# Modulation sums of a two-layer diffusion backbone: ScalarE products and accumulating transfers in place of VectorE sums

## The chip, the core and the metric

The kernel runs on one core of a Trainium2 chip. A core has a matrix engine (TensorE, PE in the profile; its weight loads are listed as PEld), VectorE (DVE), ScalarE (ACT), GpSimd (POOL) and SyncE (SP), each with an instruction stream of its own that is worked off in order; they wait for each other through semaphores. Transfers are issued from an engine's queue and carried by 16 DMA engines that all queues share. The metric is the device time of one execution in microseconds.

## What is computed

Two layers over 512 latent and 256 context tokens of width 1024: bidirectional retention, then a chunked gated MLP. Before each layer the tokens are normalised and modulated with shift, scale and gate, which come from a conditioning vector:

```python
silu_c = jax.nn.silu(c)
for i in range(DEPTH):                                   # DEPTH = 2
    shift_x, scale_x, gate_x = jnp.split(silu_c @ ada_w[i] + ada_b[i], 3, axis=-1)
    hx = rmsnorm(x, norm_g[i]) * (1 + scale_x[:, None]) + shift_x[:, None]
    ...                                                  # i = 0: retention, i = 1: gated MLP
    x = x + gate_x[:, None] * out_x
return rmsnorm(x, final_g)
```

All is float32. The products `silu_c @ ada_w` that are not needed at once, layer 0's gate and layer 1's shift, scale and gate (1024 columns each), are the subject here.

## The kernel before, in words

In the large matrix products each operand is split into a high and a low part, and three partial products are summed: a weight tile `raw` (128x1024) comes in, ScalarE casts it to the high part of `hl`, VectorE subtracts to get the low part, and PE multiplies both (24 matmuls of 128x256 per tile and product). Products are grouped seven to a quad, by a scheme that saves one product in eight; some tiles are differences of two raw ones, formed on VectorE in place. After products ScalarE copies PSUM banks to `snap` tiles (11 buffers), which GpSimd's queue stores to DRAM (`spill`, line 142). SyncE's queue brings in all weights (`load`, line 145), in order.

Beside this main work runs a generator, `background` (line 882), a step at a time (`step`, line 927, called from the loop over quads at line 1044, and from `attend` and `project_out`). It works in four pieces: gate of layer 0, shift, scale and gate of layer 1. In each, `ada_piece` (line 846) brings eight rows of 128x1024 weights (`adag_d`, 512 KB each) into slots `bg`, two to a piece, one load per step, and adds them up, each scaled by a column of `cpad` (one number per partition), in the tile `a` (`ada_a` in the profile). The sum over the 128 partitions follows on PE in `columns` (line 864) for pieces 0 to 2: matmuls of `ones` with `a` into PSUM, a copy to `cole`, transposes, a copy to `gate0`, `sh1` or `gs1`. Piece 3 casts and splits `a` into `ada_h` and multiplies that by ones. Piece 3 runs with the attention of heads 0 and 1 and uses the slots `w2` and `w3`, pieces 0 to 2 run with the projections and use `g2` and `g3`, with `a` in `g1`.

What sets the order: a scheduler lays out each engine's stream before the run by its own estimates. Matmuls keep the order of the text. On ScalarE and VectorE an instruction of a background step is held behind the one before it in the text (`aside`, line 920), the rest is free. SyncE's and GpSimd's streams are laid out freely; where a load's slot isn't free yet, the queue waits there, and what stands behind waits with it.

In `attend` (line 1060) `score` makes `pf` on VectorE, ScalarE casts it to `ph`, VectorE subtracts `pl`; PE multiplies both with `v`; `finish` sums squares and `gated` makes `gt`, which PE transposes.

Of the kernel before, what the change touches and what calls it, by code (L numbers as in the profile page):

```python
# [9 lines left out]
AF = mybir.ActivationFunctionType  # L10
ALU = mybir.AluOpType
# [56 lines left out]
def hybrid_kernel(ctx, tc, xT_d, cT_d, cv_d, sv_d, rows_d, ada0_d, adag_d, w_d, rope_d, dec_d, ws_d, id_d, out_d):  # L68
    nc = tc.nc
    pe, act, dve, sp = (Queue(tc, e) for e in (nc.tensor, nc.scalar, nc.vector, nc.sync))  # L70
# [11 lines left out]
    def st(shape, tag, dt=F32, bufs=1, name=None):  # L82
        return sb.tile(shape, dt, tag=tag, name=name or tag, bufs=bufs)
# [60 lines left out]
    def load(dst, src):  # L144
        sp.dma_start(dst, src)
# [340 lines left out]
    cpad = st([P, KT, 32], "cpad")  # L486
# [355 lines left out]
    def bg_raw(tags):  # L842
        spot[0] += 1
        return st([P, 1024], tags[spot[0] % len(tags)], name="bg")

    def ada_piece(i, tag, tags):
        a = st([P, D], tag, name="ada_a")
        rows = []
        for k in range(KT + 1):
            if k < KT:  # L850
                rows.append(bg_raw(tags))
                load(rows[k], adag_d[8 * i + k])
            if k == 0:
                yield None
                continue
            r, c = rows[k - 1], cpad[:, k - 1, 0:1]
            if k == 1:
                dve.tensor_scalar(a, r, c, None, ALU.mult)
            else:
                dve.scalar_tensor_tensor(a, r, c, a, ALU.mult, ALU.add)  # L860
            yield None
        yield a

# [18 lines left out]
    def background():  # L882
        for i in range(4):
            a = None
            for a in ada_piece(i, *(("g1", ("g2", "g3")) if i < 3 else ("oA22", ("w2", "w3")))):
                if a is None:
                    yield
# [750 lines left out]
```

## Time and profile before

| | |
|---|---|
| time, median of 3 runs | 871.4 us (870.92 to 871.57) |
| the profiled execution, first to last instruction | 869.6 us |
| granted clock of TensorE over the span, mean | 0.998 |
| bytes moved by DMA | 153.81 MB, mean 177 GB/s |
| ScalarE casts of 128x1024 weights `hl<-raw` | 197, 203.0 us in all |

In the profile a row of a timeline has start, length, engine, line, operation, out<-in, shapes, how many, and in brackets the idle time before it and what ended it. Nearly all instructions have line 54, since a helper records them; they are told apart by the names of their tiles. A row of a tile's answer has the shortest, median and longest duration in ns, and the first and last start. A DMA row has the queue that issues it, the number, the size, and the median time from issue to landing. "SPq L54 <- DVE x" tells what SyncE's queue waited for: us in all, times, longest.

### The profile page before, as it was taken

What the parts mean: (1) busy time and instruction counts of PE and PEld (TensorE: products, weight loads), DVE (VectorE), ACT (ScalarE), POOL (GpSimd) and SP (SyncE); (2) the same over time, 40 slices, a digit from 0 to 9 for tenths busy, and PEclk for the clock granted to TensorE, in tenths of its full rate; (3) what the DMA queues carried; (4) which work ended last, traced back from release to release, by engine and by line L of the source; (5) the groups of instructions that cost most, each with busy time, mean ns of one, the idle gap of its engine ahead of it and who ended that gap; (6) DMA issues with size and microseconds to landing.
All of it is one profiled execution on the core that took longest, in us unless ns stands there. A gap on an engine that the chain in (4) does not pass through costs nothing.

```text
span 869.6 us, 16989 instructions
## 1 busy us (share of the span) xinstructions
PE 860.9 (99%) x6898; PEld 824.1 (95%) x6898; DVE 715.0 (82%) x1004; ACT 458.5 (53%) x711; POOL 58.3 (7%) x96
## 2 busy tenths in 40 slices
PE   8999999999999999999999999999999999999997
PEld 7899999999999999999989899999999899899986
DVE  4799988699789777878676679999899488688995
ACT  5476644435544346627363549744666456255434
POOL 0001210101102011000000002011000000000110
PEclk9999999999999999999999999999999999999999
DMA  9943887557567467746164602635435035035522
GB/s 359 404 152 109 256 279 254 170 181 242 203 213 256 132 219 302 267 165 241 66 222 141 215 4 110 211 117 206 135 122 193 26 122 203 16 122 170 120 46 102
DMA packets 74238, 153.81 MB, mean 177 GB/s; under 512 B 7728, under 2 KB 32816, under 8 KB 74160
## 3 DMA queue, kind: packets, MB, share of 16 engines
q1 hardware_dynamic: 65856, 128.40, 43.7%
q0 software_dynamic: 7872, 24.12, 8.2%
q8 instruction: 54, 0.88, 0.4%
q14 instruction: 24, 0.20, 0.1%
q10 hardware_dynamic: 432, 0.20, 0.1%
HBM read 128.58 MB, written 24.12 MB: 176 GB/s over the span
## 4 chain that ended last, share of the span: by engine, by line
PE 95%; DMA 3%; DVE 1%; ACT 0%; issue 0%; SPq 0%; DVEq 0%; ACTq 0%
PE pst L54 95%; DMA ada_w<-in_ada_dram 2%; DMA xs<-in_xT_dram 1%; DVE o L54 0%; ACT junk L54 0%; SPq L54 0%; ACT fss L54 0%; ACT o L54 0%; DVE fss L54 0%; ACT oA L54 0%; DVE oA L54 0%; DVE xs L54 0%; DVEq L1634 0%; DVE gs L54 0%; DVE ada_s L54 0%
## 5 line engine op out<-in xcount | busy, mean ns | idle before, releaser
L54 DVE TENSOR_TENSOR hl<-raw,hl 128x1024 fp32r<-128x1024 f32 (+2 forms) x197 | 235.4, 1199 | 65.9 <-ACT hl L54 65.3
L54 ACT CAST hl<-raw 128x1024 fp32r<-128x1024 f32 (+2 forms) x197 | 203.0, 1034 | 137.9 <-DVE raw L54 55.8
L54 PE MATMUL pst<-hl,oS 128*128 128x256 f32 x1152 | 133.9, 277 | 0.0
L54 PEld LDWEIGHTS pst<-hl,oS 128*128 128x128 f32 x1152 | 132.4, 188 | 0.4 <-issue 0.4
L54 PE MATMUL pst<-oS,hl 128*128 128x256 f32 x1104 | 132.5, 277 | 0.0
L54 PEld LDWEIGHTS pst<-oS,hl 128*128 128x128 f32 x1104 | 128.1, 188 | 0.8 <-issue 0.8
L54 PE MATMUL pst<-oA,hl 128*128 128x256 f32 x936 | 116.5, 279 | 0.1
L54 PEld LDWEIGHTS pst<-oA,hl 128*128 128x128 f32 x936 | 110.6, 188 | 2.3 <-issue 0.8
L54 DVE TENSOR_TENSOR raw<-raw 128x1024 f32<-128x1024 f32 x92 | 111.8, 1219 | 0.8
L54 ACT COPY snap<-pst 128x512 f32<-128x512 f32 x92 | 53.7, 584 | 92.7 <-PE pst L54 92.4
L54 PE MATMUL pst<-hl,oA 128*128 128x256 f32 x768 | 92.4, 277 | 0.0
L54 PE MATMUL pst<-og,hl 128*128 128x256 f32 x768 | 91.1, 278 | 0.0
L54 PEld LDWEIGHTS pst<-og,hl 128*128 128x128 f32 x768 | 89.2, 188 | 0.3
L54 PEld LDWEIGHTS pst<-hl,oA 128*128 128x128 f32 x768 | 89.4, 188 | 0.0
L54 PE MATMUL pst<-v,ph 128*128 128x512 f32 x192 | 59.8, 393 | 0.0
L54 PE MATMUL pst<-hl,ya 128*128 128x512 f32 (+1 forms) x246 | 59.1, 386 | 0.0
L54 PEld LDWEIGHTS pst<-hl,ya 128*128 128x128 f32 x246 | 45.3, 188 | 9.5
L54 DVE TENSOR_TENSOR snap<-pst,snap 128x512 f32<-128x512 f32 x69 | 47.3, 685 | 5.3 <-PE pst L54 5.3
L54 PE MATMUL pst<-hl,hc 128*128 128x256 f32 x384 | 46.1, 276 | 0.0
L54 PEld LDWEIGHTS pst<-hl,hc 128*128 128x128 f32 x384 | 44.7, 188 | 0.0
L54 ACT CAST ph<-pf 128x512 fp32r<-128x512 f32 x24 | 14.8, 618 | 54.5 <-DVE pf L54 54.1
L54 PEld LDWEIGHTS pst<-v,ph 128*128 128x128 f32 x192 | 36.1, 188 | 7.1
(186 smaller groups left out, 1022.7 us busy)
## 6 DMA issues: line engine op xcount, KB each, us to landing
raw<-in_w_dram SPq DMA_DIRECT2D x224, 256.0 KB, 4.1
bg<-in_adag_dram SPq DMA_DIRECT2D x32, 512.0 KB, 3.9
ada_w<-in_ada_dram SPq DMA_DIRECT2D x16, 512.0 KB, 8.7
raw<-in_w_dram SPq DMA_DIRECT2D x16, 512.0 KB, 4.3
bg<-in_dec_dram SPq DMA_DIRECT2D x12, 512.0 KB, 4.8
v<-snap POOLq DMA_DIRECT2D x16, 256.0 KB, 5.5
z<-snap POOLq DMA_DIRECT2D x16, 256.0 KB, 4.7
v<-v SPq DMA_DIRECT2D x8, 512.0 KB, 3.4
```

The costliest lines, as they stand in the source:

```text
L54: made = op(*args, **kw)
```

## The change

Row 0 is loaded into the tile of the sum itself and scaled there by ScalarE; rows 1 to 7 are scaled in place by ScalarE, and each is added to the sum by a transfer of GpSimd's queue that accumulates into it, from SBUF to SBUF.

```diff
             if k < KT:
-                rows.append(bg_raw(tags))
+                rows.append(a if k == 0 else bg_raw(tags))
                 load(rows[k], adag_d[8 * i + k])
-            if k == 0:
-                yield None
-                continue
-            r, c = rows[k - 1], cpad[:, k - 1, 0:1]
-            if k == 1:
-                dve.tensor_scalar(a, r, c, None, ALU.mult)
-            else:
-                dve.scalar_tensor_tensor(a, r, c, a, ALU.mult, ALU.add)
+            if k:
+                r = rows[k - 1]
+                act.activation(r, r, AF.Copy, scale=cpad[:, k - 1, 0:1])
+                if k > 1:
+                    nc.gpsimd.dma_start(a, r, accum_op=ALU.add)
             yield None
```

The streams shift at many places; three are shown. The number behind a tile's name is that of the buffer's use and differs between the two programs. The first is GpSimd's queue during piece 0, before (`v`, `vc`, `q` and `z` are stores of the projections of heads 0 and 1), with what each waits for (DMASW: an earlier transfer of this queue, DMAHW: a load of SyncE's):

```order
L142 DMA vc1_220<-snap_1698 256x1x256 [waits DMASW7_49,Activation_49]
L142 DMA q01_192<-rope_a_1771 128x512 [waits DMASW0_49,DVE_49]
L142 DMA z11_226<-snap_1596 256x1x256 [waits DMASW1_49,Activation_49]
L142 DMA z10_225<-snap_1638 256x1x256 [waits DMASW2_49,Activation_49]
L142 DMA v11_214<-snap_1809 256x1x256 [waits DMASW3_49,Activation_49]
L142 DMA v10_213<-snap_1843 256x1x256 [waits DMASW4_49,DVE_49]
```

and after:

```order
L142 DMA vc1_220<-snap_1697 256x1x256 [waits DMASW7_49,Activation_49]
L857 DMA ada_a_1564<-bg_1604 128x1024 [waits DMASW0_49,DMAHW0_49,PE_49,Activation_49]
L142 DMA q01_192<-rope_a_1771 128x512 [waits DMASW1_49,DVE_49]
L142 DMA z11_226<-snap_1595 256x1x256 [waits DMASW2_49,Activation_49]
L142 DMA z10_225<-snap_1637 256x1x256 [waits DMASW3_49,Activation_49]
L857 DMA ada_a_1564<-bg_1700 128x1024 [waits DMASW4_49,DMASW0_49,Activation_49]
L142 DMA v11_214<-snap_1810 256x1x256 [waits DMASW5_49,Activation_49]
L857 DMA ada_a_1564<-bg_1778 128x1024 [waits DMASW6_49,DMASW4_49,Activation_49]
L857 DMA ada_a_1564<-bg_1813 128x1024 [waits DMASW7_49,DMASW6_49,Activation_49]
L857 DMA ada_a_1564<-bg_1872 128x1024 [waits DMASW7_49,Activation_49]
L142 DMA v10_213<-snap_1845 256x1x256 [waits DMASW1_49,DVE_49]
```

Five transfers of the sum stand between stores that followed each other before, and each waits for the transfer of the row before it.

The second is ScalarE's stream during piece 2, in the projections of head 2 and 3, before (casts of weights, and copies of PSUM banks that PE writes to again later):

```order
L54 CAST hl_3288<-raw_2836 128x1024
L54 CAST hl_3381<-raw_3114 128x1024
L54 COPY snap_3349<-pst_3322 128x512
L54 CAST hl_3319<-raw_2836 128x1024
L54 CAST hl_3426<-raw_2904 128x1024
L54 COPY snap_3410<-pst_3385 128x512
L54 CAST hl_3462<-raw_2907 128x1024
L54 COPY snap_3456<-pst_3322 128x512
```

and after:

```order
L54 CAST hl_3302<-raw_2848 128x1024
L54 ACTIVATE bg_3225<-bg_3225,cpad_175 128x1024
L54 ACTIVATE bg_3298<-bg_3298,cpad_175 128x1024
L54 CAST hl_3334<-raw_2848 128x1024
L54 CAST hl_3397<-raw_3126 128x1024
L54 COPY snap_3364<-pst_3337 128x512
L54 ACTIVATE bg_3330<-bg_3330,cpad_175 128x1024
L54 CAST hl_3443<-raw_2916 128x1024
L54 COPY snap_3426<-pst_3401 128x512
L54 ACTIVATE bg_3391<-bg_3391,cpad_175 128x1024
L54 CAST hl_3479<-raw_2919 128x1024
L54 COPY snap_3473<-pst_3337 128x512
```

The products of rows 3 to 6 (`bg`) stand between the casts and copies that the main products need.

The third is SyncE's queue during piece 3, between the attention of heads 0 and 1, before (`bg` are rows 3, 5 and 6 of the sum, `qk` and `raw` belong to the main work):

```order
L54 DMA bg_4664<-in_adag_dram 128x1024 [waits DMAHW2_49,DVE_49]
L54 DMA bg_4726<-in_adag_dram 128x1024 [waits DMAHW3_49,DMAHW2_49,DVE_49]
L54 DMA bg_4918<-in_adag_dram 128x1024 [waits DMAHW4_49,DVE_49]
L54 DMA qk_5387<-q30_197 128x512 [waits DMAHW5_49,DMASW7_49,PE_49]
L54 DMA raw_4875<-in_w_dram 128x1024 [waits DMAHW6_49,DVE_49]
```

and after:

```order
L54 DMA bg_4682<-in_adag_dram 128x1024 [waits DMAHW2_49,DMASW2_49,Activation_49]
L54 DMA bg_4746<-in_adag_dram 128x1024 [waits DMAHW3_49,DMASW3_49,Activation_49]
L54 DMA bg_4939<-in_adag_dram 128x1024 [waits DMAHW4_49,DMASW4_49,Activation_49]
L54 DMA qk_5411<-q30_197 128x512 [waits DMAHW5_49,PE_49]
L54 DMA raw_4896<-in_w_dram 128x1024 [waits DVE_49]
```

The places are the same; the loads of rows now wait for transfers of GpSimd's queue (DMASW) where they waited for VectorE.

## The prediction

> **What bounds the kernel now.** I read the busy times first, then the chain that ended last, then the stages in which the background sums run. The first row is the page's span; the second is its engine row.
>
> ```profile
> span 869.6 us, 16989 instructions
> PE 860.9 (99%) x6898; PEld 824.1 (95%) x6898; DVE 715.0 (82%) x1004; ACT 458.5 (53%) x711; POOL 58.3 (7%) x96
> ```
>
> TensorE (PE) is busy for all but 9 us. The chain of work that ended last, in order of time, says that it also waits for nobody in between (start, length, what):
>
> ```profile
> 35.69 0.12 issue
> 35.81 822.47 PE pst L54 x6564
> 858.28 0.02 issue
> ```
>
> From 35.81 to 858.28 us the chain is one unbroken run of matmuls. So nothing that VectorE (DVE) is spared in this stretch shortens the span; the change can only add to it, and only where a matmul comes to wait. The busy times by stretch, for three of the places where the background sums run (PE, PEld, DVE, ACT, POOL, granted clock, DMA share, GB/s):
>
> ```profile
> 115.00:160.00 45.00, 45.00 (x401) 44.61 (x399) 38.97 (x39) 19.74 (x26) 7.88 (x12) 1.00 0.78 259
> 240.00:280.00 40.00, 40.00 (x358) 39.57 (x356) 37.79 (x47) 18.89 (x25) 4.60 (x8) 1.00 0.71 235
> 360.00:420.00 60.00, 60.00 (x458) 56.97 (x457) 49.55 (x78) 32.29 (x52) 0.00 (x0) 1.00 0.60 213
> ```
>
> PE is full, the clock is full, ScalarE (ACT) has half its time free, and the DMA engines are already 0.60 to 0.78 busy.
>
> **What is removed and added.** The answers on the sums' tile and on the loads of their rows:
>
> ```profile
> L54 DVE SCALAR_TENSOR_TENSOR ada_a<-bg,cpad,ada_a x28: 1273/1279/1289, 119.3 to 405.1; 128x1024 f32<-128x1024 f32 x28
> L54 DVE TENSOR_SCALAR ada_a<-bg,cpad x4: 744/748/799, 114.8 to 352.5; 128x1024 f32<-128x1024 f32 x4
> L54 PE MATMUL pst<-ada_a,ones x24: 379/391/403, 159.6 to 279.8; 128*32 128x256 f32 x24
> SPq L54 <- DVE ada_a L54: 91.9, 27, 13.2
> ```
>
> VectorE loses 28 x 1.279 + 4 x 0.748 = 38.8 us. I count that at nothing: it lies beside PE's unbroken run. ScalarE gets 32 products; a 128x1024 ScalarE pass takes 1.05 us in the rows quoted below, so 34 us, also beside PE, in an engine 53% busy. GpSimd (POOL) gets 28 issues at about the 0.85 us of its accumulating transfers, 24 us on an engine 7% busy. The 32 row loads stay as they are, 512 KB each. None of these sums matters. What matters is **latency**: a sum was 1.3 us per row; it now is a transfer per row, and each waits for the one before, because all add into one tile. The slot of a row comes free not when VectorE has read it (the SyncE queue waited 27 times for that) but when its transfer has landed.
>
> **The price D of one accumulating transfer.** No 512 KB accumulating transfer is in the trace, nor one from SBUF. Nearest are the eight of 256 KB at the end (o<-x) and the plain stores of 256 KB (x<-xs); then the row loads. For each, the issue row with its median, and the minimum, median and maximum to landing, in that order:
>
> ```profile
> o<-x POOLq DMA_DIRECT2D x8, 256.0 KB, 4.0
> DMA to landing us min/median/max: 3.8/4.0/5.5
> x<-xs POOLq DMA_DIRECT2D x8, 256.0 KB, 2.7
> DMA to landing us min/median/max: 2.3/2.7/4.1
> bg<-in_adag_dram SPq DMA_DIRECT2D x32, 512.0 KB, 3.9
> DMA to landing us min/median/max: 3.2/3.9/6.9
> ```
>
> Accumulating costs 4.0 - 2.7 = 1.3 us over a plain store of 256 KB. Twice the bytes should cost that again: 5.3 us with quiet queues. The row loads, which share the engines with the weights, lie at the median 3.9 - 3.2 = 0.7 us above their quiet minimum; with that, **D = 6.0 us**. The ends: not under 3.8 (half the size, quiet), not over 2 x 5.5 = 11.0. I take 6.0 because it is the 256 KB row plus two measured steps. A row load is L = 3.9, its median.
>
> **Where PE comes to wait.** A piece is eight rows: row 0 is scaled in place, rows 1 to 7 are scaled and added. Pieces 0 to 2 end in matmuls on the sum, at 159.6, 220.7 and 279.5 us; the fourth is first read by the cast at 418.4.
>
> ```profile
> L54 ACT CAST ada_h<-ada_a x1: 1047/1047/1047, 418.4 to 418.4; 128x1024 fp32r<-128x1024 f32 x1
> 122.28 0.68 POOL L142 DMA_DIRECT2D vc<-snap  x1 [1.94 <-ACT snap L54]
> 128.09 0.63 ACT L54 ACTIVATE snap<-snap 128x512 f32<-128x512 f32 x1 [0.67 <-DVE snap L54]
> 129.02 0.68 POOL L142 DMA_DIRECT2D z<-snap  x1 [2.26 <-ACT snap L54]
> 203.69 0.62 ACT L54 ACTIVATE snap<-snap 128x512 f32<-128x512 f32 x1
> 204.73 0.71 POOL L142 DMA_DIRECT2D z<-snap  x1
> 220.72 0.64 PE L54 MATMUL pst<-ada_a,ones 128*32 128x256 f32 x8
> 238.58 0.58 ACT L54 COPY snap<-pst 128x512 f32<-128x512 f32 x1 [1.26 <-PE pst L54]
> 239.07 1.05 ACT L54 CAST hl<-raw 128x1024 fp32r<-128x1024 f32 x1
> 279.54 0.64 PE L54 MATMUL pst<-ada_a,ones 128*32 128x256 f32 x8
> ```
>
> Piece 0: row 2's product stands on ACT behind the row at 128.09, and its transfer on POOL behind the one at 129.02, so it goes out at about 130.2 (row 1's, behind the store at 122.28, has landed by 129.2). Rows 2 to 7 are six transfers in a row: 130.2 + 6 x 6.0 = 166.2. PE wants the sum at 159.6: **6.6 us**. The loads (3.9, plus 1.05 for the product) fit inside two transfers and don't set the pace.
>
> Piece 1: its steps stand wider apart, so transfers wait for the text, not for each other, until row 5, behind the rows at 203.69 and 204.73: 205.5 + 3 x 6.0 = 223.5 against 220.7: **2.8 us**.
>
> Piece 2: row 1's product ends 1.05 us after the copy at 238.58 (239.1), at 240.2; two transfers end at 252.2. Row 3 sits in row 2's slot here, so its load starts then: + 3.9 + 1.05 = 257.1, and five transfers more end at 287.1 against 279.5: **7.6 us**. The products wait on ACT in order: those of rows 5 and 6 hold up the copies behind them, but by less than the 7.6, so that isn't added.
>
> Piece 3 is not limited by its end but by the queues. The rows are ACT's, SyncE's, DVE's and PE's around 368 to 401 us:
>
> ```profile
> 367.70 1.98 ACT L54 CAST v<-v 128x1024 fp32r<-128x1024 f32 x2
> 386.11 0.33 SPq L54 DMA_DIRECT2D raw<-in_w_dram  x1
> 389.79 1.05 ACT L54 CAST hl<-raw 128x1024 fp32r<-128x1024 f32 x1 [0.20 <-DMA raw<-in_w_dram]
> 393.93 0.62 ACT L54 CAST ph<-pf 128x512 fp32r<-128x512 f32 x1 [3.09 <-DVE pf L54]
> 398.47 1.41 DVE L54 SCALAR_TENSOR_TENSOR gt<-pst,ss,z 128x512 f32<-128x512 f32 x2
> 400.67 1.03 PE L54 MATMUL pst<-ident,gt 128*128 128x128 f32 x8
> ```
>
> Row 2's product ends 1.05 us after the casts at 369.7, at 370.8; its transfer lands at 376.8. Row 3 loads then: 381.8 with its product. Transfers 3 and 4 land at 387.8 and 393.8. On SyncE the load of row 6 waits for transfer 4, and the weight load that went out at 386.11 stands behind it: 393.8 + 0.3 + 3.9 = 398.0. The cast of that weight (1.05) and row 5's product (1.05) follow on ACT, so the cast of the scores that began at 393.93 begins at 400.1, 6.2 us late. What comes of it, the gated output, was ready at 399.88 and wanted at 400.67, a cover of 0.8: 6.2 - 0.8 = **5.4 us**. A second wait, of row 7's product, moves along with this one and isn't added.
>
> Sum: 6.6 + 2.8 + 7.6 + 5.4 = 22.4 us. The span of 869.6 becomes 892.0. The profiled execution's span lies 1.8 us under the median of the runs, 871.4; with the same 1.8 the run becomes **893.8 us**. Each microsecond of D counts some 20 times, so D is the whole question.
>
> [...]
>
> **The rivals.**
> Hidden after all (not slower). If D is under 4.2 us no piece is late: six transfers from 130.2 end by 155.4, and from 240.2 two, a load and five end by 274.6; piece 3's scores then begin at 394.7, inside the cover. Up to 4.7 the lateness stays within 1.7 us, about 0.2%, which is what a measurement of this kernel can tell from no change. For it: the source lies in SBUF instead of DRAM, and the quiet 256 KB ones took 3.8. Against: 512 KB can't be quicker than 256, and the engines are 0.71 busy. It gives 871.4 us. [...]
>
> Crowded out. The 28 transfers move 14.7 MB more and, if each reads both operands, load the DMA engines twice over, in stretches already 0.71 to 0.78 busy. Then D = 7.5 and L = 5.0 (the row loads reached 6.9). The same four sums give 16 + 9 + 19 + 15 = 59 us: 931 us. For it: two overlapping accumulating transfers took 5.5 where one took 3.8. Against: PE's waiting holds back the weight loads as well.
>
> Faster. The 38.8 us of DVE would have to be on the path; the unbroken run of matmuls says that they aren't. Only the last 10 us, which the change doesn't touch, wait for DVE.
>
> **How the numbers follow.** Forecast (D from 4.7 to 7.2): 0.74, likeliest 893.8. Hidden: 0.12. Crowded out: 0.12. Faster: 0.02. D = 5.0 gives 0.6 + 0 + 0.7 + 2.4 = 3.7 us, 875; D = 7.2 with L = 5 some 51 us, 922. The range reaches a little below the first and over the second, 872 to 925; it leaves out the hidden case and the upper half of the crowded one, 0.18. Faster 0.02, same 0.12, slower 0.86.
>
> **What would show it.** In the changed profile: the transfers ada_a<-bg with a median to landing near 6; SyncE waiting for them; idle time of PE ended by the DMA ada_a<-bg just before the matmuls on the sum in pieces 0 to 2, some 7, 3 and 8 us; ACT's wait before the product rows, ended by row loads; DVE's busy time near 676 us and no gain from it; in piece 3 a weight load that starts after 390 in the old frame. A median of 4.5 or less, with PE without gaps, makes the forecast wrong; so does one of 7 or more, with gaps of 15 us.

## The result, and the profile after

The changed kernel takes **929.65 us** (median; 928.0 to 932.28) against 871.22 before: 1.0671 times, 95% interval 1.065 to 1.0693, or 58 us slower. The prediction was 893.8 with a range of 872 to 925: the direction is right, the size isn't. The profiled execution has a span of 926.3 us, 56.7 more than before.

First the page of the changed kernel: the span, the engines' busy times, and of the DMA issues the median time from issue to landing of row loads and transfers.

```profile
span 926.3 us, 17045 instructions
PE 878.2 (95%) x6898; PEld 838.9 (91%) x6898; DVE 680.8 (73%) x972; ACT 490.9 (53%) x743; POOL 83.4 (9%) x124
bg<-in_adag_dram SPq DMA_DIRECT2D x28, 512.0 KB, 3.9
ada_a<-bg POOLq DMA_DIRECT2D x28, 512.0 KB, 6.9
```

PE has the same 6898 matmuls as before, but it is idle for 926.3 - 878.2 = 48.1 us (8.7 before, so 39.4 more), and it is *busy* for 17.3 us more (878.2 - 860.9). The two are the whole 56.7. A transfer takes 6.9 us where I took 6.0; a row load takes the 3.9 that I took.

The idle time first. The waits of PE in the changed kernel: who waited for whom, us in total, times, the longest.

```profile
PE pst L54 <- ACT snap L54: 16.3, 4, 6.2
PE pst L54 <- DMA ada_a<-bg: 10.9, 3, 5.7
PE pst L54 <- DVE snap L54: 5.2, 1, 5.2
PE pst L54 <- DVE pl L54: 4.9, 1, 4.9
PE pst L54 <- DVE acc L54: 2.7, 2, 1.7
```

Together 40.0 us. Only 10.9 of it is named after the transfers; the largest row names a copy of ScalarE out of PSUM. ScalarE's own order of time shows what stands behind that (start, length, what, and in brackets the idle time ahead of it with what ended it), with the queue of SyncE, which issues the loads, and its waits below it:

```profile
304.32 1.15 ACT L54 ACTIVATE bg<-bg,cpad 128x1024 f32<-128x1024 f32 x1 [4.28 <-DMA bg<-in_adag_dram]
305.38 1.03 ACT L54 CAST hl<-raw 128x1024 fp32r<-128x1024 f32 x1
306.31 0.57 ACT L54 COPY snap<-pst 128x512 f32<-128x512 f32 x1
```

```profile
300.23 0.33 SPq L54 DMA_DIRECT2D bg<-in_adag_dram  x1
```

```profile
SPq L54 <- DMA ada_a<-bg: 154.3, 26, 11.7
```

The copy at 306.31 is what PE waited for until 306.94. Ahead of it in ScalarE's queue stands a product that waited 4.28 us for its row; the row's load went out only at 300.23, because SyncE held it (26 such waits, 154.3 us) until the transfer out of the same slot had landed. So this wait, the longest of the row "ACT snap", comes from a transfer too, three steps back.

Now the busy time. The matmuls are as many as before, so they were slower. Four stretches of 3.4 us around a gap of the first piece (stretch, its length, busy time and instructions of PE, PEld, DVE, ACT, POOL, then the granted clock, the DMA engines' share and GB/s):

```profile
154.07:157.48 3.41, 0.00 (x0) 0.00 (x0) 0.21 (x1) 2.08 (x2) 0.00 (x0) 1.00 1.06 250
157.48:160.90 3.42, 1.66 (x8) 1.69 (x9) 3.39 (x4) 1.22 (x2) 1.62 (x2) 0.50 1.01 347
160.90:164.31 3.41, 3.41 (x18) 3.41 (x18) 3.38 (x4) 1.63 (x3) 0.69 (x1) 0.50 1.06 265
164.31:167.72 3.41, 3.41 (x31) 3.41 (x30) 1.51 (x3) 3.25 (x5) 0.95 (x2) 1.00 0.57 203
```

PE stood still from 154.07 to 159.24. From 157.48 to 164.31 the granted clock is 0.50, and in a full stretch PE makes 18 matmuls at that clock and 31 behind it. The wait was paid as a wait and once more, in part, as slow work after it.

The profile has six such stretches beside PE's waits, five of 6.83 us and one of 3.41, and PE is busy for 27.3 us in them. Against the same matmuls of the kernel before, its busy time is some 14 us longer inside them and 3.3 us longer outside. Of these 3.3 some 1.8 lie in the first 11 us, long before the first sum, where a matmul on `xs` took 421 ns at the median and 273 before; they aren't the sums'. So the clock is some 14 of the 17.3 us.

### The profile page after: what moved, and what is told of

Same layout as the page of the kernel before. It is cut to its first block, busy times and chain, and to the rows that moved or that the text cites. A ratio compares the mean times of both kernels' runs of the same rounds, so it can differ in the third digit from the quotient of the medians.

```text
span 926.3 us, 17045 instructions
## 1 busy us (share of the span) xinstructions
PE 878.2 (95%) x6898; PEld 838.9 (91%) x6898; DVE 680.8 (73%) x972; ACT 490.9 (53%) x743; POOL 83.4 (9%) x124
## 3 DMA queue, kind: packets, MB, share of 16 engines
q1 hardware_dynamic: 65856, 128.40, 41.8%
q0 software_dynamic: 11904, 38.80, 15.9%
## 4 chain that ended last, share of the span: by engine, by line
PE 47%; DMA 2%; ACT 1%; DVE 1%; issue 0%; DVEq 0%; ACTq 0%; SPq 0%
PE pst L54 47%; DMA bg<-in_dec_dram 1%; DMA ada_a<-bg 1%; ACT bg L54 0%; DMA bg<-in_adag_dram 0%; ACT junk L54 0%; DVE o L54 0%; DVE v L54 0%; ACT L54 0%; ACT fss L54 0%; DVE acc L54 0%; DVE dt L54 0%; ACT o L54 0%; DVE fss L54 0%; ACT qk L54 0%
## 5 line engine op out<-in xcount | busy, mean ns | idle before, releaser
L54 PE MATMUL pst<-hl,oS 128*128 128x256 f32 x1152 | 140.1, 284 | 16.6 <-ACT snap L54 16.3
L54 PEld LDWEIGHTS pst<-hl,oS 128*128 128x128 f32 x1152 | 137.7, 195 | 18.2 <-ACT snap L54 17.1
L54 PE MATMUL pst<-oA,hl 128*128 128x256 f32 x936 | 118.5, 282 | 0.0
L54 PEld LDWEIGHTS pst<-oA,hl 128*128 128x128 f32 x936 | 112.6, 191 | 2.6 <-issue 1.2
L54 PE MATMUL pst<-hl,oA 128*128 128x256 f32 x768 | 94.9, 282 | 5.2 <-DVE snap L54 5.2
L54 PEld LDWEIGHTS pst<-hl,oA 128*128 128x128 f32 x768 | 91.9, 192 | 5.3 <-issue 5.3
L54 ACT ACTIVATE bg<-bg,cpad 128x1024 f32<-128x1024 f32 x28 | 32.0, 1151 | 53.3 <-DMA bg<-in_adag_dram 53.3
```

Source lines behind the costliest of these rows:

```text
L54: made = op(*args, **kw)
```

## The experiments

Theory at the start: the chain of transfers, 6.9 us each and one behind the other, makes rows, products and sums late, and PE's gaps lower its clock besides. Rivals: ScalarE's 32 new passes; the two slots; the load on the DMA engines; something in the transfers that lowers the clock.

### The products alone

```
-                    nc.gpsimd.dma_start(a, r, accum_op=ALU.add)
+                    dve.tensor_tensor(a, a, r, ALU.add)
```

> ScalarE forms the products in place as in the change, but VectorE adds them (28 additions of 128x1024, some 1.2 us each); no accumulating transfer is left. Theory (the transfers' latency is the cost): the products hide in an engine that is 53% busy, PE has no gap over 1 us before 850 us, and the time is that of before within 0.2%, 871.2 (869.5 to 873). Rival (32 products of 1.15 us in ScalarE's queue, each of which waits in order for a row, hold up the copies that PE waits for by themselves): gaps ended by ScalarE's copies stay, some 15 to 29 us, and the time is 886 to 900.

Measured: 872.62 us, 1.0012 times before (1.0003 to 1.0021), some 1 us, and PE has no gap over 0.2 us between 10 us and the end of its work. Moving the products to ScalarE costs next to nothing. The loss is in the transfers.

### Four slots for the rows

```
-            for a in ada_piece(i, *(("g1", ("g2", "g3")) if i < 3 else ...
+            for a in ada_piece(i, *(("g1", ("g2", "g3", "g0", "s3")) if i < 3 else ...
```

> As the changed kernel, but in pieces 0 to 2 the rows rotate through four tiles instead of two, so that a row's load no longer waits for the transfer of the row two before it. Theory A (the chain of transfers, 6.9 us each, one behind the other, is itself too long): PE's gaps ended by ScalarE's copies go (there are four of 2.0 to 6.2 us and one ended by its cast), but the lateness shows up at the matmuls on the sums instead: 123.2 + 7 x 6.9 = 171.5 against 159.6, about 12 us in piece 0, then 5 and 9, with 7.6 in piece 3, some 34 us of gaps, and the clock is again at half after them: 910 to 922. Rival B (the two tiles are the cost: loads wait for transfers and ScalarE waits for loads): with the tiles the transfers keep up with the steps, pieces 0 to 2 lose nothing, piece 3 keeps its 7.6 us and one stretch at half clock: 880 to 884.

Measured: 930.85 us (1.0686, 1.066 to 1.0712), no better than the change. PE's two longest waits in this kernel:

```profile
PE pst L54 <- DMA ada_a<-bg: 36.4, 3, 14.4
PE pst L54 <- DVE pl L54: 5.6, 1, 5.6
```

The waits for ScalarE's copies are gone but for 0.2 us, as theory A has it, and the waits for the sums rose from 10.9 to 36.4 us. The lateness is in the chain; the slots only decide where PE meets it. My number for the time was too low by 9 us: the gaps at the sums were 13.3, 8.7 and 14.4 us, not 12, 5 and 9.

### Each transfer in two halves

```
-                    nc.gpsimd.dma_start(a, r, accum_op=ALU.add)
+                    for c in range(0, D, 512):
+                        nc.gpsimd.dma_start(a[:, c:c + 512], r[:, c:c + 512], accum_op=ALU.add)
```

> As the changed kernel, but each accumulating transfer is issued as two of 256 KB, one for each half of the columns; the halves don't wait for each other. Theory A (the 6.9 us are mostly a latency of one transfer, of which two run side by side): a half lands in 4 to 5 us as the 256 KB ones at the end of the kernel did (4.0), the pair in 5 to 6, and the sum of gaps falls from 39.8 to between 5 and 23 us: 876 to 905. Theory B (they are bytes over what the DMA engines give to two rows read and one written): the pair lands in 7 us or more, the second half 0.9 us later still for its issue, and the time is 926 or more.

Measured: 929.17 us (1.0659, 1.0642 to 1.0677): theory B's number.

```profile
ada_a<-bg POOLq DMA_DIRECT2D x56, 256.0 KB, 5.7
```

A half takes 5.7 us, where the whole took 6.9 and the eight 256 KB transfers at the kernel's end 4.0. From the issue of the first half to the landing of both a pair takes 7.4 us at the median (computed from the trace), so two at a time gain nothing here. Theory B's reason, the bytes, is tested below with half of the columns.

### Gaps of PE without transfers

```
         act.copy(e, pr)
-        yield
+        for _ in range(n):  # n = 2, 5, 10 in pieces 0, 1, 2
+            nc.gpsimd.tensor_copy(e, e)
         pq = pt((P, 2, P), tag="tm")
...
         dve.tensor_copy(dst.rearrange("p (j b) -> p j b", j=4), v[:, 0, :, :])
+        yield
```

> The kernel before, with no accumulating transfer in the sums; in the column step of pieces 0, 1 and 2 GpSimd copies the 128x256 intermediate onto itself 2, 5 and 10 times before PE may transpose it, which makes three gaps of PE of rising length (what one copy takes isn't in the trace; the lengths are to be read from it). Theory (it is the idle time itself that lowers PE's clock): after a gap of 3 us or more the granted clock is 0.5 for 3.4 or 6.8 us, after one under 1.5 us it isn't, and the span grows by the gaps and by half of the time at 0.5. Rival (the clock fell in the changed kernel because of what the transfers or the DMA engines do): the clock stays at 1.0 and the span grows by the gaps alone.

Measured: 894.35 us (one run). The three gaps are 2.59, 5.30 and 9.69 us, 17.6 together, and the span grew by 892.6 - 869.6 = 23.0: the other 5.4 us I put down to the clock, whose mean over the span is 0.987 (0.998 before). The stretches around the shortest gap (160.29 to 162.88), then those around the longest (292.87 to 302.56), columns as above:

```profile
158.90:162.30 3.40, 1.39 (x15) 0.77 (x14) 1.60 (x2) 1.32 (x2) 1.12 (x1) 1.00 0.52 162
162.30:165.70 3.40, 2.82 (x13) 2.82 (x14) 0.33 (x2) 0.00 (x0) 0.46 (x2) 0.50 0.60 184
165.70:169.10 3.40, 3.40 (x31) 3.40 (x30) 0.09 (x1) 1.53 (x2) 0.00 (x0) 1.00 0.00 0
```

```profile
292.00:295.41 3.41, 0.87 (x11) 0.26 (x9) 3.20 (x4) 2.41 (x5) 2.90 (x5) 1.00 0.54 169
295.41:298.83 3.42, 0.00 (x0) 0.00 (x0) 3.42 (x4) 1.04 (x1) 3.30 (x3) 0.50 0.61 217
298.83:302.24 3.41, 0.00 (x0) 0.00 (x0) 1.09 (x1) 0.00 (x0) 3.04 (x7) 0.50 0.32 76
302.24:305.65 3.41, 3.09 (x15) 3.09 (x16) 0.50 (x3) 0.00 (x0) 0.27 (x1) 0.50 0.00 1
305.65:309.07 3.42, 3.42 (x32) 3.42 (x32) 0.00 (x0) 0.59 (x1) 0.00 (x0) 1.00 0.02 5
```

No transfer adds to a sum in this kernel, and the clock is 0.50 all the same, for 3.40 us (162.30 to 165.70) in and behind the gap of 2.59 us and for 10.24 us (295.41 to 305.65) in and behind that of 9.69. In this run the gaps were enough without such transfers.

### Matmuls put into two of the gaps

```
         pr = pt((P, HS), tag="tm")
+        for _ in range(n):  # n = 0, 8, 16 in pieces 0, 1, 2
+            mm(pr[:, 0:P], ones, ones, start=True, stop=True)
```

> The changed kernel with 8 and 16 matmuls of 128x128 (0.275 us each, on a tile of ones) put ahead of the matmuls on the sums of pieces 1 and 2, into the PSUM tile that these overwrite: 2.2 us into a gap of 3.10 and 4.4 us into one of 5.66. Theory (PE's idle time costs twice: once itself, once through the clock): both gaps end where they ended, at the landing of the sum's last transfer, what is left of them is 0.9 and 1.3 us, no stretch at 0.5 follows them, and PE has 3.4 / 2 + 6.8 / 2 = 5.1 us less to do: 924.5 against 929.65. Rival (the clock isn't what the rest of the loss is): the matmuls fill idle time and the time stays at 929 to 930.

Measured: 928.42 us (1.0648, 1.0629 to 1.0667): the interval overlaps that of the change, so the time tells nothing. The two gaps shrank from 3.13 to 0.95 and from 5.69 to 2.49 us. But elsewhere gaps grew (2.08 us at the sum of piece 0, now 3.30; 1.67 at 476 us, now 2.32), and the mean granted clock over the span is 0.978, against 0.979 in the change: the time at the low clock didn't shrink on the whole. Inconclusive as a cure.

### Half of the columns

```
-                    nc.gpsimd.dma_start(a, r, accum_op=ALU.add)
+                    nc.gpsimd.dma_start(a[:, 0:512], r[:, 0:512], accum_op=ALU.add)
```

> The changed kernel, in which the transfers add only columns 0 to 511 of each row (28 transfers of 256 KB in place of 512 KB; the other columns of the sums are left out). Loads, products and order stay. Theory (the time of one transfer, D, is the lever: by the prediction's steps D = 6.9 gives 40 us of gaps, 6.0 some 22, 5.0 some 4, 4.5 none): a transfer lands in 4.3 to 5.2 us, gaps come to 0 to 6 us, the clock falls at most once, 871 to 879. Rival (the issue on GpSimd, the waits for its semaphores or ScalarE's place in the order hold PE up, whatever a transfer takes): gaps of over 15 us stay and the time is above 890.

Measured: 898.64 us (1.0312, 1.0286 to 1.0337). My expectation failed at its first step: half the bytes take not 4.3 to 5.2 us but nearly as long as the whole.

```profile
ada_a<-bg POOLq DMA_DIRECT2D x28, 256.0 KB, 5.6
DMA to landing us min/median/max: 3.2/5.6/8.5
```

So the bytes are not the larger part of D: half of them is worth 1.3 us of 6.9. That speaks against theory B's reason for the halves too. At 5.6 us for a transfer the time is 31 us below the change's: D is a lever, but halving the transfer is a poor way to move it. Gaps of 19.4 us together stay and the time is above 890, which is the rival's number. The run doesn't decide against the rival, since the transfers didn't become as short as its test needs.

### The fourth piece alone

```
-            if k:
+            if k and i == 3:
                 r = rows[k - 1]
                 act.activation(r, r, AF.Copy, scale=cpad[:, k - 1, 0:1])
...
+            elif k:  # pieces 0 to 2 as in the kernel before
```

> The fourth piece alone by products and transfers; pieces 0 to 2 by VectorE as before. Theory (the four pieces cost apart from each other): gaps of 4.9, 1.7 and 1.0 us as in the changed kernel, one stretch of 6.8 us at half clock after the longest, 7.6 + 3.2 = 10.8 us: 882. Rival (the fourth piece's loss comes with the lateness of the first three, whose loads of decay rows and weights were late when it began): under 2 us of gaps, 871 to 873.

Measured: 883.38 us (1.0137, 1.012 to 1.0153), 12 us.

```profile
PE pst L54 <- DVE pl L54: 6.7, 1, 6.7
PE pst L54 <- DVE acc L54: 2.5, 2, 1.4
```

By itself the fourth piece has no shorter gaps than in the change (there 4.9 and 2.7), so its loss doesn't come with the lateness of the first three. If the pieces add up, 0 to 2 cost the remaining 929.65 - 883.38 = 46 us.

### The pieces spread, its control, and more slack

Two steps for each row and a step behind each product of a projection, the fourth piece by VectorE:

```
             yield None
+            if i < 3 and k:
+                yield None
...
-            if 2 not in pieces and i not in (2, 4):
+            if 2 not in pieces:
```

> Pieces 0 to 2 by products and transfers, but with two steps for each row and a step behind each of the seven products of a projection instead of five, so that a row comes some 8 us after the one before it instead of some 6; the fourth piece by VectorE as before. All 21 transfers of those pieces are still made. Theory (nothing but the pace is wrong: 6.9 us of transfer, one behind the other, in 6 us of steps): no gap of over 1.5 us is left, VectorE's busy time is 715 - 3 x 9.7 = 686 us, and the time is that of before, 871 to 874. Rival (the transfers cost by their load on the DMA engines and on ScalarE's order, whatever their pace): gaps of over 8 us stay and the time is above 882.

Measured: 888.87 us (1.0198, 1.0166 to 1.023): well down from 929.65, but the rival's number, not mine. Its longest waits of PE:

```profile
PE pst L54 <- DVE snap L54: 4.4, 1, 4.4
PE pst L54 <- DVE rope_a L54: 3.8, 1, 3.8
PE pst L54 <- ACT snap L54: 3.0, 1, 3.0
```

The row that names `rope_a` ended just ahead of the matmuls on a sum, at 255.59; the last transfer into that sum had gone out at 245.7 and taken 9.7 us.

With a third slot (the tile w7) and one more step ahead of the column step:

> The spread kernel (two steps for each row of pieces 0 to 2, the fourth piece by VectorE), with a third tile for the rows and one more step between the last row and the matmuls on the sum. The 21 transfers and products stay. In the spread kernel three gaps were left, 3.0, 3.7 and 4.4 us, together with the clock 17.5 us: a copy of ScalarE behind a product that waited 7.3 us for its row, a sum whose last transfer took 9.8 us, and a copy of VectorE. Theory (these come where single transfers take 8 to 11 us, beyond the slack of a step, and end with more slack): at most one gap over 1.5 us, 871 to 877. Rival (traffic or ScalarE's 21 more passes cost, whatever the slack): gaps of together over 8 us stay and the time is 884 to 889.

Measured: 888.40 us (1.0206, 1.0189 to 1.0223): no gain, and the rival's number again (gaps of 11.6 us together). The gap of 3.0 us behind ScalarE's copy is gone, a longer one (5.1) stands elsewhere:

```profile
PE pst L54 <- DVE snap L54: 5.1, 1, 5.1
```

Ahead of that gap ScalarE waited 9.6 us for a *decay* row, a load of another stage that ran beside a transfer and six weight loads. And the schedule alone, with VectorE's sums and no transfer:

> The kernel before in the spread kernel's schedule (two steps for each row of pieces 0 to 2, a step behind each product), sums by VectorE, without any transfer. Theory (the 17.5 us that the spread kernel still loses come from its 21 transfers): no gap over 1.5 us, 871 to 873. Rival (the schedule itself, which puts the pieces beside the decay rows and the first queries, makes that loss): gaps of over 5 us and 877 to 889.

Measured: 874.34 us (1.003, 1.0017 to 1.0042), one gap of 1.3 us: 2.4 us over the kernel before. So of the spread kernel's 17.5 us some 2.4 are the schedule's and 15 go with the products and transfers. Pace takes away two thirds of the loss of pieces 0 to 2, not all.

### Without most of the row loads

```
-                rows.append(a if k == 0 else bg_raw(tags))
-                load(rows[k], adag_d[8 * i + k])
+                rows.append(a if k == 0 else bg_raw(tags) if k < 3 else rows[k - 2])
+                if k < 3:
+                    load(rows[k], adag_d[8 * i + k])
```

> The changed kernel without the loads of rows 3 to 7 of each piece (20 loads of 512 KB are left out; the products of rows 1 and 2 are multiplied on in their tiles, so all products and all 28 transfers of 512 KB stay). Theory (the 2 us by which a transfer exceeded its quiet 4.5 us come from what else the DMA engines carry, the row loads first): a transfer takes 5.0 to 5.8 us at the median, gaps come to 0 to 15 us, 872 to 893. Rival A (they come from the weights' loads and the stores, which stay): 6.5 us or more, gaps over 20 us, above 897. Rival B (the rows' loads, by their own 3.9 us between two transfers, hold the products up, and the transfers' time is no matter): gaps under 5 us though the median stays above 6.5.

Measured: 894.45 us (1.0259, 1.0242 to 1.0277), a microsecond above the upper end of the theory's range; the median transfer is at its upper end too.

```profile
ada_a<-bg POOLq DMA_DIRECT2D x28, 512.0 KB, 5.8
PE pst L54 <- DMA ada_a<-bg: 14.7, 3, 6.0
```

Taking 20 loads of 512 KB out of the engines goes with transfers that are 1.1 us shorter (5.8 against 6.9): company on the engines is a part of D. The gaps stand at the sums (6.0, 3.4, 5.3 us) but for one of 1.0 us. Not all of the 35 us gained is D's: without loads, the products of rows 3 to 7 no longer wait for a load either. And weights and stores still run beside the transfers.

### The transfers with nobody waiting for them

First try: beside each of VectorE's 21 additions, a transfer from the rope table to a tile that nobody reads.

```
                 dve.scalar_tensor_tensor(a, r, c, a, ALU.mult, ALU.add)
+                if i < 3:
+                    nc.gpsimd.dma_start(extra, rope.rearrange("p a n -> p (a n)"), accum_op=ALU.add)
```

> The kernel before, with VectorE's sums, and beside each of the 21 additions of pieces 0 to 2 an accumulating transfer of 512 KB from the rope table to a tile that nobody reads, in GpSimd's queue where the change has its own. The load on the DMA engines and the waits in GpSimd's queue are there, and no row, product or sum waits for a transfer. Theory (the changed kernel's loss in these pieces is the chain of dependent transfers): a transfer takes 6 to 7.5 us, gaps of under 4 us together, 871 to 876. Rival (the load itself, which makes weights, rows and stores late, is most of it): gaps of over 10 us, above 884.

Measured: 921.75 us (1.0582, 1.0556 to 1.0607), and it doesn't answer the question. Nothing tied the transfers to their steps, so they stood in GpSimd's queue in a row, each waiting for the one before, and the stores of the projection behind them:

```profile
206.16 0.83 POOL L865 DMA_DIRECT2D extra<-rope  x1 [4.71 <-DMA extra<-rope]
210.94 0.84 POOL L865 DMA_DIRECT2D extra<-rope  x1 [3.94 <-DMA extra<-rope]
211.48 0.87 POOL L142 DMA_DIRECT2D k<-rope_a  x1
216.17 0.69 DVE L54 TENSOR_TENSOR rope_b<-snap,rope 128x512 f32<-128x512 f32 x1 [19.56 <-DMA k<-rope_a]
```

The store of k went out behind them at 211.48, VectorE waited 19.56 us for it, and PE, which waited for VectorE, stood still from 201.45 for 23.2 us. It shows what waiting transfers can do to a queue that they share, in an order that the changed kernel doesn't have.

Second try: each transfer is released by its row's addition.

```
+                if i < 3:
+                    j = 7 * i + k - 2
+                    dve.tensor_copy(mark[:, j:j + 1], a[:, 0:1])
+                    nc.gpsimd.tensor_copy(source[:, 0:1], mark[:, j:j + 1])
+                    nc.gpsimd.dma_start(extra, source, accum_op=ALU.add)
```

> The kernel before, with VectorE's sums; for each of the 21 additions of pieces 0 to 2, GpSimd's queue carries an accumulating transfer of 512 KB between two tiles that nobody reads. Unlike in the run before, each is released by its row's addition (by way of a word that VectorE copies and GpSimd writes into the source), so that the 21 keep the pace and the places that the change gives them. No row, product or sum waits for one. Theory (the changed kernel's loss in pieces 0 to 2 is that rows and sums wait for the transfers): gaps of under 4 us together, 871 to 876. Rival (what the transfers do to others, in the DMA engines and in GpSimd's queue, is most of it): gaps of over 10 us, above 884.

Measured: 875.52 us (1.0056, 1.0038 to 1.0073), 4.5 us. Its issues, with the median to landing, then two stretches of the first pieces, and the same two in the changed kernel:

```profile
bg<-in_adag_dram SPq DMA_DIRECT2D x32, 512.0 KB, 5.5
extra<-source POOLq DMA_DIRECT2D x21, 512.0 KB, 6.3
```

```profile
115.00:160.00 45.00, 45.00 (x400) 44.45 (x398) 39.43 (x46) 19.93 (x26) 13.88 (x19) 1.00 0.92 266
190.00:230.00 40.00, 40.00 (x356) 39.46 (x355) 34.56 (x45) 17.08 (x23) 11.40 (x20) 1.00 0.99 295
```

```profile
115.00:160.00 45.00, 37.82 (x328) 37.46 (x327) 23.13 (x26) 22.05 (x27) 11.35 (x15) 0.97 0.89 254
190.00:230.00 40.00, 35.35 (x312) 35.15 (x310) 23.79 (x30) 18.08 (x22) 9.59 (x13) 0.99 0.81 224
```

The DMA engines are busier than in the change (0.92 and 0.99 against 0.89 and 0.81), the transfers take nearly as long (6.3 against 6.9), and PE is full in these stretches; its gaps come to 2.9 us. The load costs 4.5 us; of the 46 us of pieces 0 to 2 the rest comes only when rows and sums wait for the transfers. The granted clock is 1.00 in these stretches and 0.998 over the span, as before, with all 21 transfers: in this run they didn't lower it.

### Two sums in turn

```
-                rows.append(a if k == 0 else bg_raw(tags))
+                rows.append(sums[k] if k < n else bg_raw(tags))  # sums: ada_a and a second tile
...
-                if k > 1:
-                    nc.gpsimd.dma_start(a, r, accum_op=ALU.add)
+                if k > n:
+                    nc.gpsimd.dma_start(sums[(k - 1) % n], r, accum_op=ALU.add)
...
+            if len(sums) > 1:
+                dve.tensor_tensor(a, a, sums[1], ALU.add)
```

> The kernel with four tiles for the rows, in which even rows are added to one tile and odd ones to a second, three transfers each; VectorE adds the two tiles ahead of the matmuls on the sum. A transfer waits for the one two before it, not the one before it. Pieces 0 to 2 make 18 transfers in place of 21; the fourth piece is the change's. Theory (one behind the other is the cost): two at a time take 7 to 9 us each, so that a row costs 3.5 to 4.5 us of chain against a step of some 6; pieces 0 to 2 keep gaps of at most 5 us together, and with the fourth piece's 12 us (the run of that piece alone) the time is 883 to 892. Rival (the DMA engines and not the chain set the pace): the pairs take 12 us or more, and the time stays above 905.

Measured: 903.0 us (1.0362, 1.0345 to 1.0379), between the two. PE's waits at the sums:

```profile
PE pst L54 <- DVE ada_a L54: 13.1, 3, 6.7
```

They fall from 36.4 us (four slots, one sum) to 13.1. That the chain is what they come from, as the theory says, fits this; but each piece also has one transfer less, which at 6.9 us each could be most of the 23 us, and the run doesn't tell the two apart. What is left in piece 0 is no chain: the last transfer went out at 155.72, behind its product (154.29), when the one before it on its tile (140.06, 8.7 us) had long landed, and took 9.6 us by itself. No run here beats the kernel before, and the profile leaves little room for it: PE was busy for all but 9 us of it.

## Why the prediction was wrong, point by point

**The bound** was right: what VectorE was spared (34 us on the page: 715.0 to 680.8, where I had said 676) bought nothing, and the 32 products on ScalarE cost about 1 us of the time. A product took 1.15 us, not 1.05. The missing 4.6 us are a matter of counting: summed instruction by instruction VectorE does 39.1 us less (773.9 and 734.8), near my 38.8, but the page counts the time in which one instruction overlaps the next only once.

**The price D** was the term that was mis-sized. I had put it together from 4.0 for 256 KB, 1.3 for twice the bytes, and 0.7 for company on the DMA engines, the last read from the row loads (median less minimum). Two transfers of the changed kernel to compare, 190.41 to 194.98 and 212.66 to 221.85 (columns as above, the clock and the DMA share near the end):

```profile
190.40:194.98 4.58, 4.58 (x43) 4.58 (x42) 3.39 (x5) 2.00 (x2) 0.88 (x1) 1.00 0.60 114
212.66:221.85 9.19, 9.19 (x83) 9.19 (x83) 6.86 (x8) 3.70 (x5) 3.42 (x5) 1.00 1.04 337
```

The first has the engines to itself (114 GB/s over 4.58 us are its own 512 KB) and takes 4.6 us, below my 5.3 for the quiet case. The second, at a DMA share of 1.04 and 337 GB/s, takes twice as long, 9.2. So the size step was, if anything, too dear, and the step "with that, D = 6.0", which added **0.7 us** for company, is the one that failed: company costs 6.9 - 4.6 = 2.3 us at the median. The loads of the kernel before were no measure for it: in the changed kernel their median stayed at 3.9 while the transfers lost 2.3. (Where 21 transfers run and no load waits for them, the loads lose too: 5.5.) Halving the bytes fits: 3.2 at the quietest, 5.6 at the median.

**The four sums** hold as working. With 6.9 in place of 6.0 the same steps give: piece 0, 130.2 + 6 x 6.9 - 159.6 = 12.0; piece 1, 205.5 + 3 x 6.9 - 220.7 = 5.5; piece 2, 257.1 + 2 x 0.9 + 5 x 6.9 - 279.5 = 13.9; piece 3, three transfers more to 0.9 each, 5.4 + 2.7 = 8.1. Together 39.5 us; PE's gaps in the trace are 9.3, 8.6, 14.5 and 7.6, 40.0. That the totals agree so well is in part luck, since pieces 0 and 1 are off by 3 us in opposite directions. The 0.9 us in D are 17 of the 34 us that the forecast of the span lacked (926.3 - 892.0), much as "some 20 times" says. That the products' waits on ScalarE "aren't added" was right for the sum, though not for the place: PE met most of the lateness where ScalarE copies and VectorE adds out of PSUM (16.3 and 5.2 us), before it reached the sums, where only 2.1, 3.1 and 5.7 us were left of the 7, 3 and 8 that I had announced. Four slots moved it to the sums.

**The clock** was missing altogether. I added PE's waits to the span as if PE went on at full speed behind them. It lost some 14 us more in the stretches at 0.50, most of the other half of the error. No rival had it either, and the range ended at 925.

**Piece 3** began as described. The work there stands 46.9 us later than before (the cast of scores at 381.02 is now at 427.93), so the weight load of 386.11 was due at 433.0. SyncE's rows and ScalarE's:

```profile
432.45 6.76 SPq L54 DMA_DIRECT2D bg<-in_adag_dram  x2
439.73 0.42 SPq L54 DMA_DIRECT2D raw<-in_w_dram  x1
```

```profile
445.28 1.04 ACT L54 CAST hl<-raw 128x1024 fp32r<-128x1024 f32 x1 [8.80 <-DMA raw<-in_w_dram]
446.23 1.14 ACT L54 ACTIVATE bg<-bg,cpad 128x1024 f32<-128x1024 f32 x1
448.22 0.62 ACT L54 CAST ph<-pf 128x512 fp32r<-128x512 f32 x1 [0.84 <-DVE pf L54]
```

The weight went out at 439.73, behind the row's load that waited; its cast waited 8.80 us, and the cast of the scores came at 448.22 where 393.93 + 46.9 = 440.8 was due: 7.4 us late (I had 6.2). PE met 4.9 us of that, at the matmuls with `pl` at 449.62 and not at the gated output. The 2.7 us ahead of the output products are another matter. The chain of work that ended last (start, length, what) shows where they come from:

```profile
447.67 6.58 DMA ada_a<-bg
454.30 3.66 DMA bg<-in_adag_dram
464.58 10.47 DMA bg<-in_dec_dram
```

A transfer landed, row 7's load went out behind it, row 7's product ran on ScalarE at 458.04, and behind that a load of decay rows took 10.47 us (5.3 at the median), beside the last transfer, which went out at 466.29; PE went on at 480.31. "A second wait, of row 7's product, moves along with this one and isn't added" was thus wrong by up to 2.7 us, and the nearness of 8.1 to 7.6 is in part luck. Alone the piece costs 12 us with the clock.

**The rivals.** "Hidden" and "faster" are out: the median is 6.9, not under 4.7, and the quietest of the 28 took 4.5 (3.2 with half of the columns). "Crowded out" gave 931 us and the run 929.65, but its conditions (D = 7.5, L = 5.0, 59 us of waits) aren't met: D is 6.9, L is 3.9 and the waits are 40 us. Its 59 us are a slip besides: with D = 7.5 and L = 5.0 the four sums give 15.6, 7.3, 19.3 and 12.0, 54 us, and with D = 7.2 some 48 in place of 51. So it is luck that its time is met: the clock, which it didn't have, adds what its waits lacked. Its reason, crowded DMA engines, is the sound one for D (9.2 us at a share of 1.04, 4.6 at 0.60), though not as a cost by itself (4.5 us). Its "twice over" comes near, with some 1.7 times: by the pages' rows of DMA queues, GpSimd's queue took 8.2% of 869.6 us before and 15.9% of 926.3 after, so that, as an estimate from these rows, a transfer fills all 16 engines for 2.7 us, where 512 KB of SyncE's loads (128.40 MB in 43.7% of 869.6 us) fill them for 1.55.

What stays open: how much of a transfer's 2.3 us comes from row loads, weights and stores apart, the 1.5 us by which PE is busier with no clock to blame, and the last 15 us of the spread kernel, whose gaps stand where single transfers and loads take 8 to 11 us, which I have read from its trace but not taken away.

## What to carry to other kernels

Price a dependent chain of transfers at the time that one takes among the traffic of its own stretch: here that was 4.6 us at a DMA share of 0.60 and 9.2 at 1.04, and neither half the bytes (5.6 against 6.9 at the median) nor the row loads' surplus (0.7 us) said much of it. Look at the granted clock behind PE's waits too: here the six of 3.13 us and more were paid for as waits and again, in part, as slow work (30.6 us of idle time, some 14 of longer busy time), while those of 2.57 us and less left the clock at 1.00. And look for the cause of a wait elsewhere than where it is met: of the changed kernel's 40.0 us PE met 16.3 at ScalarE's copies, and the longest of these, 6.2 us, led back through the queues to a transfer.

## What the runs showed of the hardware that I had not expected

In the changed kernel the granted clock of PE is 0.50 for 6.83 us with gaps of 5.18, 5.44, 6.24, 5.69 and 4.91 us and for 3.41 us with one of 3.13; in the run with gaps and no transfers it is 0.50 for 3.40 us with a gap of 2.59 and for 10.24 us with one of 9.69. It can begin while PE still waits (157.48 in a gap from 154.07 to 159.24). The length of the gap alone doesn't tell: 2.59 us were followed by the low clock there, and 2.57 us in the changed kernel (289.37 to 291.95) weren't. What decides it these runs don't show.

Half of the columns in an accumulating transfer saved 1.3 us of 6.9 at the median (5.6); two halves at a time on the same queue took 5.7 each.
